# Two-layer hybrid attention trunk on one core: warm-up products of 512 rounded columns, values of two head pairs in one group, and a new written-out order

## The chip, the cores and the metric

The kernel runs on one core of one Trainium2 chip. The metric is the device time of one execution in microseconds (us). Of the kernel before there are three timed executions and one profiled one.

## The reference, cut to what matters

A trunk of two layers on 256 tokens of 1024 features. Layer 0 feeds two groups of heads from one projection: A (8 heads, sliding window with sinks) and B (8 heads, three branches: compressed, selected, window). Layer 1 is block-sparse attention with 16 heads. With 256 tokens every selected block and every window covers all earlier tokens, so each of these branches is causal attention here. The values of B are the sum of three gated branches for each head:

```python
for layer in range(DEPTH):
    ada = silu(c) @ w_ada[layer] + b_ada[layer]
    shift, scale, gate = split(ada, 3)
    h = rms_norm(x, norm_g[layer]) * (1 + scale) + shift
    y = even_mixer(h, ...) if layer % 2 == 0 else odd_mixer(h, ...)
    x = x + gate * y
return rms_norm(x, final_g)

# even_mixer, B:
o = g[..., 0:1] * o_cmp + g[..., 1:2] * o_slc + g[..., 2:3] * o_win   # then * silu(zb), then w_out
```

## The kernel before, in words

Every product with weights is made in rounded fp32 (float32r) from split operands: ScalarE rounds a weight tile to `whi` (a cast), VectorE subtracts to get the rest `wlo`, activations are split in the same way into `hhi`/`hlo` and `ghi`/`glo`, and `mm3` (line 557) makes three products of each pair: high by high, high by low, low by high. Attention scores, values, transposes and the small adaLN products are in plain fp32; a plain fp32 product that is no transpose shows as two records in the trace.

`Plan` (line 183) records each instruction with its number instead of issuing it (so nearly every row of the profile has the line of the call in `record`, L276). `issue` (line 279) then issues all of them in the order of the table `ORDER`, written out by hand at the top of the file; each engine's own queue is the part of that table that belongs to it. `FLIP` lists by number the copies and scalings that go to the other one of VectorE and ScalarE. An engine works through its queue in order. The DMAs of the weights are all issued from SP.

The stages, in order of time:

- Start (lines 356 to 381 and 685 to 823). 32 warm-up products of a 128x128 tile of ones (`ones`, lines 369 to 378) stand in TensorE's queue between the first small products; nobody reads their result. Shift and scale of layer 0 are made in five groups of feature blocks (`START`, line 24). For each, DMAs bring a part of `w_ada` into tiles that are free at that time (`qT`, `gate`, `oT`, `kTb`, `t`), VectorE adds up the first few of its rows into `acc`, and TensorE adds the rest in a group of tiled products into bank `ps_m` (`start_sums`, line 731). With shift and scale of a block known, the block of the normed input is split, and `start_mm` (line 793) multiplies it with its rows of `w_in_even`, which come through `raw` tiles.
- Layer 0 attention (lines 834 to 1114). `attn_four` (line 609) makes the scores of two heads and two branches (`ps_s`), VectorE takes row extremes (`mn`), ScalarE the exponentials (`sm`, `den`), VectorE the reciprocals (`rc`), either of them scales, TensorE transposes (`ps_pt`), and the copies land in tiles of the ring `pT`, which has 4 tiles and 3 more out of `bigA`. `attn_values` (line 660) then multiplies with the values into bank `ps_o`; `plan.group` makes each of its products wait for what any of them needs. `b_pair` (line 1054) does this for the two heads of one pair: ten products, twenty records, one bank, one gating (`gated`) of 256 columns. Between them stand projections for the SiLU gates (`gate_path`), the compression MLP (`compress`), and VectorE's adaLN sums for later (`fill`, tiles `raw` and `acc`).
- Output projection of layer 0 and norm for layer 1 (lines 1116 to 1150), then layer 1 (lines 1152 to 1289) and its output projection, norm and stores (lines 1290 to 1330).

## Time and profile before

| | us |
|---|---|
| median of 3 runs (294.68, 294.72, 314.98) | 294.72 |
| the profiled execution | 295.43 |
| its span from first to last instruction | 293.7 |
| mean granted TensorE clock over the span | 0.996 |

The profile is of the execution that took 295.43 us; 1.73 us of that lie outside its span. In the profile PE is TensorE's matmul, PEld its weight load, DVE is VectorE, ACT ScalarE, POOL GpSimd, and SPq the queue that SP issues DMAs from. A row `ps_o<-pT,vb x16` stands for sixteen records that write a tile of `ps_o` from `pT` and `vb`; buffer numbers are left out. The time of a matmul record holds its own latency and overlaps the next one, so the pace is read from the starts, not from the durations.

### The profile page before, as it was taken

The page shows a single profiled execution, that of the slowest core. Times are in us where ns is not written, and L with a number is a line of the kernel's source. Part 1 is how long each engine was busy: PE and PEld are TensorE (multiplying, and loading weights), DVE is VectorE, ACT ScalarE, POOL GpSimd, SP SyncE. Part 2 cuts the span into 40 slices and gives each one's busy share as a digit, 9 for nine tenths or more (in the row PEclk, how much of TensorE's full clock was granted, in tenths as well). Part 3 has the DMA queues.
Part 4 walks back from the last instruction along what each step waited for, and adds up shares of the span by engine and source line. Part 5 has one row for each costly group of instructions (what it writes and reads, how often), then busy time and mean ns, then how long its engine had stood idle before and what let it go on. Part 6 is the DMA issues. An engine that isn't in the chain of part 4 may idle for free.

```text
span 293.7 us, 6077 instructions
## 1 busy us (share of the span) xinstructions
PE 283.5 (97%) x2244; PEld 243.5 (83%) x2244; DVE 253.0 (86%) x612; ACT 201.2 (69%) x513; POOL 5.5 (2%) x27
## 2 busy tenths in 40 slices
PE   8989999999999999999899999999999999999991
PEld 7868888997789888777667799999799899887891
DVE  0669999999999999999899868898699889889973
ACT  5554746695999999996398744466667377783821
POOL 2100000000000000000000000000000000000000
PEclk9999999999999999999999999999999999999998
DMA  7999999987996787799996449608927661604003
GB/s 260 364 385 377 383 355 353 311 287 237 342 400 212 264 281 293 213 323 361 305 372 216 146 143 329 243 4 296 351 71 249 237 234 34 227 27 145 1 15 129
DMA packets 50557, 71.76 MB, mean 244 GB/s; under 512 B 2792, under 2 KB 36192, under 8 KB 50528
## 3 DMA queue, kind: packets, MB, share of 16 engines
q1 hardware_dynamic: 50128, 70.95, 70.7%
q10 hardware_dynamic: 400, 0.43, 0.4%
q8 instruction: 17, 0.28, 0.4%
q14 instruction: 12, 0.10, 0.1%
HBM read 70.32 MB, written 1.06 MB: 243 GB/s over the span
## 4 chain that ended last, share of the span: by engine, by line
PE 73%; DVE 13%; DMA 8%; issue 2%; ACT 2%; SPq 0%; DVEq 0%
PE ps_pj L276 49%; PE ps_s L276 9%; PE ps_pt L276 6%; DVE raw L276 5%; PE ps_o L276 4%; PE ps_m L276 4%; DMA kTb<-in_w_ada_dram 3%; DMA raw<-in_w_ada_dram 2%; DVE wlo L276 2%; DMA qT<-in_w_ada_dram 2%; DMA xs<-in_x_dram 1%; DVE t L276 1%; DVE oT L276 1%; ACT t L276 1%; DVE bigA L276 1%
## 5 line engine op out<-in xcount | busy, mean ns | idle before, releaser
L276 ACT CAST whi<-raw 128x512 fp32r<-128x512 f32 (+2 forms) x108 | 71.6, 689 | 33.6 <-PE ps_pj L276 15.8
L276 DVE TENSOR_TENSOR wlo<-raw,whi 128x512 fp32r<-128x512 f32 (+2 forms) x92 | 70.8, 792 | 6.4 <-ACT whi L276 6.4
L276 PE MATMUL ps_pj<-hlo,whi 128*128 128x256 f32 x256 | 70.8, 284 | 0.0
L276 PE MATMUL ps_pj<-hhi,wlo 128*128 128x256 f32 x256 | 70.0, 284 | 0.3 <-DVE wlo L276 0.3
L276 PE MATMUL ps_pj<-hhi,whi 128*128 128x256 f32 x256 | 69.9, 284 | 0.0
L276 PEld LDWEIGHTS ps_pj<-hlo,whi 128*128 128x128 f32 x256 | 48.0, 189 | 0.6 <-issue 0.3
L276 PEld LDWEIGHTS ps_pj<-hhi,wlo 128*128 128x128 f32 x256 | 47.4, 189 | 0.7 <-DVE wlo L276 0.5
L276 PEld LDWEIGHTS ps_pj<-hhi,whi 128*128 128x128 f32 x256 | 47.4, 188 | 0.3
L276 ACT ACTIVATE sm<-sm,mn 128x256 f32<-128x256 f32 (+1 forms) x58 | 25.9, 449 | 6.9 <-DVE mn L276 6.9
L276 PE MATMUL ps_pj<-whi,hhi 128*128 128x512 f32 (+2 forms) x72 | 25.8, 368 | 0.5 <-ACT hhi L276 0.4
L276 PE MATMUL ps_pj<-whi,hlo 128*128 128x512 f32 (+2 forms) x72 | 26.1, 374 | 0.0
L276 PE MATMUL ps_pj<-wlo,hhi 128*128 128x512 f32 (+2 forms) x72 | 26.0, 370 | 0.0
L276 DVE SCALAR_TENSOR_TENSOR wlo<-raw,whi 128x512 fp32r<-128x512 f32 x32 | 20.6, 686 | 3.7 <-ACT whi L276 3.6
L276 PE MATMUL ps_pj<-wlo,ghi 128*128 128x512 f32 (+1 forms) x56 | 20.4, 368 | 0.0
L276 PE MATMUL ps_pj<-whi,ghi 128*128 128x512 f32 (+1 forms) x56 | 20.4, 369 | 0.0
L276 PE MATMUL ps_pj<-whi,glo 128*128 128x512 f32 (+1 forms) x56 | 20.0, 367 | 0.0
L276 ACT ACTIVATE sm<-sm,rc 128x256 f32<-128x256 f32 (+1 forms) x41 | 17.3, 449 | 2.3 <-DVE rc L276 2.3
L276 DVE SCALAR_TENSOR_TENSOR raw<-raw,cz,raw 128x1024 f32<-128x1024 f32 x14 | 17.9, 1276 | 1.0 <-DMA raw<-in_w_ada_dram 0.9
L276 DVE SCALAR_TENSOR_TENSOR acc<-raw,cz,acc 128x1024 f32<-128x1024 f32 x14 | 17.9, 1278 | 0.1
L276 PEld LDWEIGHTS ps_pj<-whi,hhi 128*128 128x128 f32 x72 | 13.6, 188 | 2.7 <-ACT hhi L276 1.2
L276 PEld LDWEIGHTS ps_pj<-whi,hlo 128*128 128x128 f32 x72 | 13.5, 188 | 2.5 <-DVE hlo L276 0.8
L276 PE MATMUL ps_pt<-ident,sm 128*128 128x128 f32 x87 | 15.5, 279 | 0.0
(252 smaller groups left out, 599.7 us busy)
## 6 DMA issues: line engine op xcount, KB each, us to landing
raw<-in_w_in_odd_dram SPq DMA_DIRECT2D x16, 1024.0 KB, 7.5
raw<-in_w_ada_dram SPq DMA_DIRECT2D x8, 1024.0 KB, 6.2
raw<-in_w_ada_dram SPq DMA_DIRECT2D x16, 512.0 KB, 5.2
raw<-in_w_in_even_dram SPq DMA_DIRECT2D x8, 652.0 KB, 7.2
raw<-in_w_in_even_dram SPq DMA_DIRECT2D x5, 1024.0 KB, 7.7
raw<-in_w_out_even_dram SPq DMA_DIRECT2D x4, 1024.0 KB, 5.4
raw<-in_w_out_odd_dram SPq DMA_DIRECT2D x4, 1024.0 KB, 5.0
qT<-in_w_ada_dram SPq DMA_DIRECT2D x12, 256.0 KB, 6.2
```

What stands on the lines that cost most here:

```text
L276: self.ops.append(dict(key=eng.key, deps=deps, fn=lambda: getattr(real, name)(*args, **kw)))
```

## The change

It has four parts.

1. The warm-up products are made in rounded fp32 and with 512 columns instead of 128, from the first 512 columns of `ghi`, which is set to one for it by VectorE (a memset of 128x512 in place of one of 128x128). Their number, 32, stays. `ones` shrinks to two columns.
2. `b_quad` takes the place of two calls of `b_pair`: the scores and softmax of two head pairs are recorded, then all their values, twenty products, in one group into the two halves of one bank, then one gating of 512 columns. Four groups of values become two. The `stop` flag is now set for each half.
3. `pT_more` makes the ring of `pT` tiles one longer (8 in layer 0); `hp` has one buffer instead of two.
4. `ORDER` and `FLIP` are written anew, so that instructions on all engines stand in another order. The numbers in it also shift by one from the eighth instruction on. By `FLIP`, eleven copies and scalings more are VectorE's and eleven fewer ScalarE's; with one memset more and two gatings fewer VectorE has 624 instructions for 614, ScalarE 422 for 433. Four of the eleven are scalings of 128x128 in layer 0's attention.

```diff
 ORDER = [int(i) for i in """
-49 7 6 4 0 1 9 21 22 23 2 3 47 5 91 41 42 48 92 89 24 25 26 27 28 29 30 93 73 88 50 31 90 32 74 99 58 33 75 34
...
+2944 2916 2919 2917 2872 2945 2946 2947 2948 2973 2974 2975 2976 2977 2980 2982 2981 2983 2978 2979
...
-    ones = const([P, P], "ones")
+    ones = const([P, 2], "ones")
+    ghi = const([P, KT, S], "ghi", F32R)
+    ones_r = ghi[:, 0:2, :].rearrange("p a b -> p (a b)")
     ring_warm = bank("m")
+    V.memset(ones_r.bitcast(F32), 1.0)
     V.memset(ones, 1.0)
     dummy = const([P, 2], "dummy")
     A.activation(dummy[:, 0:1], ones[:, 0:1], AF.Exp)
     for _ in range(WARM):
-        T.matmul(ring_warm[:, :P], ones, ones, start=True, stop=True)
+        T.matmul(ring_warm, ones_r[:, :P], ones_r, start=True, stop=True)
     keep = bank("o")
     for _ in range(20):
-        T.matmul(keep[:, :P], ones, ones, start=True, stop=True)
+        T.matmul(keep, ones_r[:, :P], ones_r, start=True, stop=True)
...
-    ghi = const([P, KT, S], "ghi", F32R)
     glo = const([P, KT, S], "glo", F32R)
...
         ids = []
+        last = {cs: n for n, (cs, keys) in enumerate(jobs)}
...
-                        stop=n == len(jobs) - 1 and m == len(keys) - 1,
+                        stop=n == last[cs] and m == len(keys) - 1,
...
     bigA = const([P, 2304], "bigA")
+    pT_more = const([P, 3 * P], "pT_more")
...
-            hp = sb([P, 256], "hp", 2)
+            hp = sb([P, 256], "hp", 1)
...
-        ks = sb([P, 256], "hp", 2)
+        ks = sb([P, 256], "hp", 1)
...
+    ring["pT"][0].append(pT_more)
...
-    def b_pair(hp_, cmp):
+    def b_pair(hp_):
         g = hp_ // 2
...
         pts = attn_four([keys(0), keys(1)], maskc, None, [gv[:, 2 * hp_ : 2 * hp_ + 2, :, 1 + br] for br in range(2)])
+        cs = S * (hp_ % 2)
+        return [(cs, cmp_keys(hp_))] + [(cs, keys_of(lambda b, br=br: vb[:, b, 3 * br + g, :], pts[br])) for br in range(2)]
+
+    def b_quad(g, mid):
+        js = b_pair(2 * g)
+        mid()
+        js += b_pair(2 * g + 1)
         po = bank("o")
-        attn_values(po, ([(0, cmp_keys(hp_))] if cmp else []) + [(0, keys_of(lambda b, br=br: vb[:, b, 3 * br + g, :], pts[br])) for br in range(2)])
-        gated(po, 4 + hp_, 1, 0.25)
-        if hp_ % 2:
-            gated_parts(3 + hp_)
-
+        attn_values(po, js)
+        gated(po, 4 + 2 * g, 2, 0.25)
+        gated_parts(4 + 2 * g)
...
-    b_pair(0, True)
-    fill(1)
-    b_pair(1, True)
+    b_quad(0, lambda: fill(1))
     fill(1)
     gate_path(W0, 2456 + 256, 6)
-    b_pair(2, True)
-    fill(1)
-    fill(1)
-    b_pair(3, True)
+    b_quad(1, lambda: fill(2))
     fill(1)
     fill(1)
```

The first place is the start, on TensorE: the rows before the second `ps_m` group of `start_sums` (tiles `kTb`, `oT` with `cz` and `acc`), which shifts and scales feature blocks 1 and 2. `whi`, `wlo`, `hhi` are split weights and inputs of block 0. Before:

```order
L276 MATMUL ps_pt_90<-whi_113,hhi 128x256
L276 MATMUL ps_o_70<-wlo_117,hhi 128x408
L276 MATMUL ps_pj_100<-whi_112,hhi 128x512
L276 MATMUL ps_pt_90<-wlo_117,hhi 128x256
L276 MATMUL ps_s_98<-ident,t_94 128x128
L276 MATMUL ps_pj_101<-wlo_116,hhi 128x512
L276 MATMUL ps_pj_100<-wlo_116,hhi 128x512
L276 MATMUL ps_s_97<-wlo_116,hhi 128x512
L276 MATMUL ps_m_68<-kTb,cz 32x128 x8
L276 MATMUL ps_m_68<-acc_111,cz 32x128 x4
```

And of the changed kernel, where a warm-up product reads `ghi`:

```order
L275 MATMUL ps_s_98<-whi_113,hhi 128x512
L275 MATMUL ps_o_71<-ghi 128x512
L275 MATMUL ps_pj_102<-whi_113,hhi 128x512
L275 MATMUL ps_o_71<-ghi 128x512
L275 MATMUL ps_pj_101<-whi_113,hhi 128x512
L275 MATMUL ps_s_99<-whi_113,hhi 128x512
L275 MATMUL ps_m_69<-oT,cz 32x128 x8
L275 MATMUL ps_m_69<-kTb,cz 32x128 x8
L275 MATMUL ps_m_69<-acc_112,cz 32x128 x4
L275 MATMUL ps_s_99<-wlo_117,hhi 128x512
L275 MATMUL ps_s_98<-wlo_117,hhi 128x512
```

Before, thirteen products of block 0 stand ahead of that group (the seven of them above and six earlier ones; together 5472 columns: six products of 512, four of 408, three of 256); now four of 512 columns do (2048 columns), all of them above, and the others stand behind it. The `oT` part of the group has moved down to the `kTb` part.

What SP issues in that time, before (`xs` is the input, `raw` holds rows of `w_in_even`; a row of 128x1304 is 652 KB, 128x384 is 192 KB, the `w_ada` pieces 256 KB each):

```order
L276 DMA xs<-in_x_dram 128x1024 x2
L276 DMA qT_104<-in_w_ada_dram 128x4x128
L276 DMA raw_106<-in_w_in_even_dram 128x1304
L276 DMA qT_103<-in_w_ada_dram 128x4x128
L276 DMA raw_106<-in_w_in_even_dram 128x384
L276 DMA qT_103<-in_w_ada_dram 128x4x128
L276 DMA qT_104<-in_w_ada_dram 128x4x128
L276 DMA oT<-in_w_ada_dram 128x2x256 x2
L276 DMA qT_105<-in_w_ada_dram 128x2x256 x2
L276 DMA gate<-in_w_ada_dram 128x2x256 x2
L276 DMA kTb<-in_w_ada_dram 128x2x256 x2
L276 DMA raw_107<-in_w_in_even_dram 128x1304
```

And now:

```order
L275 DMA xs<-in_x_dram 128x1024
L275 DMA gate<-in_w_ada_dram 128x2x256
L275 DMA qT_106<-in_w_ada_dram 128x2x256 x2
L275 DMA xs<-in_x_dram 128x1024
L275 DMA qT_104<-in_w_ada_dram 128x4x128 x2
L275 DMA qT_105<-in_w_ada_dram 128x4x128 x2
L275 DMA raw_107<-in_w_in_even_dram 128x1304
L275 DMA gate<-in_w_ada_dram 128x2x256
L275 DMA kTb<-in_w_ada_dram 128x2x256
L275 DMA oT<-in_w_ada_dram 128x2x256 x2
L275 DMA kTb<-in_w_ada_dram 128x2x256
L275 DMA raw_107<-in_w_in_even_dram 128x384
```

The second half of the input and the first weight rows go behind pieces of `w_ada`, and the 192 KB of `raw` that stood in the middle go behind the last piece of `kTb`.

The second place is layer 0's B heads. On TensorE, the values of the second pair before (`pcT` are the compressed branch's weights, `pT` and `bigA` the transposed softmax tiles, `vz` and `vb` the values):

```order
L276 MATMUL ps_pj_99<-whi_114,glo 128x512
L276 MATMUL ps_pt_90<-ident,sm_127 128x128 x3
L276 MATMUL ps_o_70<-pcT,vz 64x256 x2
L276 MATMUL ps_o_70<-bigA,vb 64x256
L276 MATMUL ps_o_70<-pT_131,vb 64x256
L276 MATMUL ps_o_70<-bigA,vb 64x128
L276 MATMUL ps_o_70<-pT_131,vb 64x128
L276 MATMUL ps_o_70<-pT_132,vb 64x256
L276 MATMUL ps_o_70<-pT_133,vb 64x256
L276 MATMUL ps_o_70<-pT_132,vb 64x128
L276 MATMUL ps_o_70<-pT_133,vb 64x128
L276 MATMUL ps_s_97<-kTb,qT_103 128x128
```

And the first half of the first quad's values now; the second half, ten more products, follows at once:

```order
L275 MATMUL ps_pj_101<-whi_115,glo 128x512
L275 MATMUL ps_pt_91<-ident,sm_128 128x128 x2
L275 MATMUL ps_o_71<-pcT,vz 64x256 x2
L275 MATMUL ps_o_71<-pT_133,vb 64x256
L275 MATMUL ps_o_71<-pT_134,vb 64x256
L275 MATMUL ps_o_71<-pT_133,vb 64x128
L275 MATMUL ps_o_71<-pT_134,vb 64x128
L275 MATMUL ps_o_71<-pT_135,vb 64x256
L275 MATMUL ps_o_71<-bigA,vb 64x256
L275 MATMUL ps_o_71<-pT_135,vb 64x128
```

And on ScalarE now, from the copy that fills the last tile the first quad needs (`pT_132`) to the copy that can start only when the quad's values have been made, since it writes a tile that they read (`pT_133`):

```order
L275 COPY pT_132<-ps_pt_91 128x384
L275 ACTIVATE bigA,den_141<-bigA,mn_138 128x256
L275 ACTIVATE sm_130,den_140<-sm_130,mn_137 128x256
L275 ACTIVATE bigA,den_141<-bigA,mn_138 128x128
L275 ACTIVATE bigA,den_141<-bigA,mn_138 128x256
L275 ACTIVATE oT<-ps_pj_100 128x512
L275 ACTIVATE oT<-ps_pj_102 128x512
L275 CAST whi_116<-raw_110 128x1024
L275 ACTIVATE bigA<-bigA,rc_144 128x256
L275 ACTIVATE sm_130<-sm_130,rc_143 128x128
L275 ACTIVATE sm_131<-sm_131,rc_143 128x256
L275 COPY pT_133<-ps_pt_91 128x384
```

Before, the group of ten products stood between scores of one pair and the next, and a copy of the following pair wrote a tile freed one pair earlier; now one tile less is free at that point.

## Rows read from the trace of the kernel before

**Rows 1.** The page: engines over the whole span.

```profile
PE 283.5 (97%) x2244; PEld 243.5 (83%) x2244; DVE 253.0 (86%) x612; ACT 201.2 (69%) x513; POOL 5.5 (2%) x27
```

**Rows 2.** Windows: length, busy PE, PEld, DVE, ACT, POOL; clock; DMA; GB/s.

```profile
18.60:50.00 31.40, 31.39 (x238) 26.43 (x239) 28.14 (x62) 17.75 (x39) 0.00 (x0) 1.00 1.07 368
50.00:102.00 52.00, 52.00 (x463) 44.82 (x461) 51.12 (x169) 45.24 (x142) 0.38 (x3) 1.00 0.88 299
102.00:125.00 23.00, 23.00 (x196) 18.22 (x196) 23.00 (x54) 22.79 (x67) 0.32 (x1) 1.00 0.75 255
125.00:146.00 21.00, 20.63 (x121) 15.55 (x119) 19.94 (x34) 14.39 (x34) 0.00 (x0) 1.00 0.95 328
146.00:166.00 20.00, 18.86 (x90) 13.20 (x90) 18.01 (x43) 17.22 (x42) 0.61 (x2) 1.00 0.82 280
166.00:287.40 121.40, 121.35 (x996) 110.75 (x996) 102.79 (x228) 72.85 (x172) 0.95 (x3) 1.00 0.48 162
```

**Rows 3.** Waits of PE over the whole span: total us, times, longest.

```profile
PE ps_m L276 <- DMA kTb<-in_w_ada_dram: 1.1, 1, 1.1
...
PE ps_s L276 <- DVE wlo L276: 0.8, 1, 0.8
PE ps_pj L276 <- ACT hhi L276: 0.4, 1, 0.4
PE ps_pj L276 <- DVE wlo L276: 0.3, 1, 0.3
```

**Rows 4.** The chain that ended last: start, length, what.

```profile
11.01 7.55 DMA kTb<-in_w_ada_dram
18.61 0.86 PE ps_m L276 x24
...
166.05 18.91 PE ps_pj L276 x152
...
266.63 20.82 PE ps_pj L276 x112
```

**Rows 5.** Timeline of the start, and one window of it.

```profile
0.90 0.17 DVE L276 MEMSET ones<- 128x128 f32 x1 [0.90 <-PEq L1386]
...
1.49 3.86 PEld L276 LDWEIGHTS ps_o<-ones 128*128 128x128 f32 x20
...
7.23 0.49 DVE L276 TENSOR_SCALAR t<-xs,r 128x512 f32<-128x512 f32 x1
...
9.45 0.75 PEld L276 LDWEIGHTS ps_m<-ones 128*128 128x128 f32 x6
...
0.00:18.56 18.56, 16.25 (x145) 14.56 (x145) 7.61 (x19) 10.15 (x19) 3.17 (x18) 1.00 0.95 328
```

**Rows 6.** Timeline of PE around one pair's values.

```profile
135.69 0.40 PE L276 MATMUL ps_pj<-wlo,ghi 128*128 128x512 f32 x1
135.93 0.40 PE L276 MATMUL ps_pj<-whi,glo 128*128 128x512 f32 x1
136.26 0.65 PE L276 MATMUL ps_o<-pcT,vz 128*64 128x256 f32 x4
136.74 1.47 PE L276 MATMUL ps_o<-pT,vb 128*64 128x256 f32 x16
138.14 0.50 PE L276 MATMUL ps_s<-whi,glo 128*128 128x512 f32 x1
138.48 0.40 PE L276 MATMUL ps_s<-whi,ghi 128*128 128x512 f32 x1
```

**Rows 7.** Groups by form, 70 to 146 us, DVE, then ACT: busy us, mean ns.

```profile
L276 DVE SCALAR_TENSOR_TENSOR oT<-ps_o,oT 128x256 f32<-128x256 f32 x4 | 1.7, 419 | 0.0
L276 DVE SCALAR_TENSOR_TENSOR oT<-ps_o,oT 128x512 f32<-128x512 f32 x2 | 1.4, 688 | 0.0
...
L276 DVE TENSOR_SCALAR sm<-sm,rc 128x128 f32<-128x128 f32 x2 | 0.6, 280 | 0.0
L276 ACT CAST whi<-raw 128x1024 fp32r<-128x1024 f32 x12 | 12.4, 1043 | 2.3 <-PE ps_pj L276 2.0 <-DMA raw<-in_w_out_even_dram 0.3
L276 ACT ACTIVATE sm<-sm,mn 128x256 f32<-128x256 f32 x15 | 7.5, 503 | 2.3 <-DVE mn L276 2.3
```

257 rows, old and new, of tables (FLIP, ORDER) are left out of this document.

## The prediction

> **What bounds the kernel now.** I read the page's first part, the windows by stage, the waits of TensorE, the chain that ended last, and then the timeline where a step needs a pace. The page gives PE 97% of the span [rows 1]. The windows say what stands beside it: from 18.6 to 125 us PE is full, and from 50 to 125 us VectorE is full with it, 74.1 of 75 us [rows 2]. From 166 to 287.4 us PE is full alone, and VectorE has 18.6 us to spare. The waits of PE are few: 1.1 us for the DMA of `kTb` in the start, and 0.8, 0.4 and 0.3 us for VectorE and ScalarE [rows 3]. The chain fits: a DMA until 18.56 us, then TensorE's work, and from 166.05 to 287.45 us TensorE's again [rows 4]; between them it goes through VectorE.
>
> So layer 1 can give nothing but by fewer products, and the change takes none of these away. What can move is the start before 18.6 us, the amount of TensorE's and VectorE's work from there to 166 us, and about 1.5 us of waits at the layer's end.
>
> **Warm-up products.** They go from 32 plain products of 128 columns, 64 records, to 32 rounded ones of 512. At the later pace an old record takes 0.11 us: six loads take 0.75 us with the last one's own latency in it [rows 5]. That is 64 x 0.11 = 7.0 us. A rounded product of 512 columns takes 0.24 us from start to start [rows 6], so 32 x 0.24 = 7.7 us. In the first 4 us records stand 3.86 / 20 = 0.19 us apart on average [rows 5], and the new products should be slower in the same ratio; the page's granted clock shows no step there. The difference lies between 0 and 0.7 us. The memset before the first of them grows from 0.17 us; four times that is 0.66, an operation of VectorE over 128x512 took 0.49 [rows 5], so it is up to 0.5 us later. I cost both at nothing: the cover is the wait of the second `ps_m` group for `kTb`, which becomes longer than its 1.1 us by the products that no longer stand ahead of it. Without that cover they cost up to 1.2 us.
>
> **Start, the new order.** Behind 18.6 us PE is never idle until 125 us, so a product that was made before that group and is now made after it is time lost, unless the group comes sooner. Nine products of block 0 move behind it, 5472 - 2048 = 3424 columns: 3424 / 512 x 0.24 = 1.6 us later. What comes sooner: up to the last piece of `kTb` SP issued 4,940 KB (1,024 of `xs`, 12 x 256 of `w_ada`, 652 + 192 of `raw`), and now 4,748 KB, since 192 KB of `raw` go behind it. At 368 GB/s [rows 2] that is 0.53 us. But when `kTb` had landed, 18.56 us x 328 GB/s = 6.1 MB had moved [rows 5], 1.0 MB more than what was issued up to it, so transfers behind it had run beside it, and the gain can be as little as 0. The trace has no row between; I take the middle, 0.3.
>
> The Trainium skill (page "DMA: Bandwidth & Descriptors", section "Queues, rings and completion order") says that completion is not in the order of issue for one issuing engine. By that the group comes no sooner and the start costs 1.6 us; by strict order it would cost 1.1. The 6.1 MB agree with the page.
>
> The second half of the input is issued behind 768 KB of `w_ada`. Its square and scaling come later, but its transposes stand behind the first `ps_m` group now, and the wait for `kTb` is behind them too: nothing. Sum for the start: 1.6 - 0.3 = +1.3 us.
>
> **Values in one group.** One pair's values take 1.88 us, 136.26 to 138.14. Ahead of them the start-to-start time is 0.33 us where 0.24 is the pace, behind them 0.34: 0.09 + 0.10, so 0.2 us for entering and leaving a group [rows 6]. Four groups become two: -0.4 us of PE. The products themselves stay.
>
> On VectorE four gatings of 256 columns at 0.419 us become two of 512 at 0.688: -0.3 us. Four scalings of 128x128 come over from ScalarE at 0.28 each: +1.1 [rows 7]. So VectorE has 0.8 us more in a stretch in which it is full, and ScalarE four instructions less.
>
> TensorE is then 1.3 - 0.4 = 0.9 us later at the layer's end and VectorE 0.8 us. They run side by side, so I count the later one, +0.9, not the sum. If the two hit each other instead of lying side by side, it is up to 1.7.
>
> **A buffer more for `pT`, one less for `hp`.** A copy into `hp` now waits until the two small products that read the tile are done. The trace shows no such wait; two products of 512 columns would be 0.5 us, and 0 is the other end. Behind it on ScalarE wait exponentials and casts for TensorE. I take 0, because TensorE has products of a projection in its queue there and never waits from 50 to 102 us. The first copy for the third pair must wait for the whole first quad. In the order ScalarE has ten instructions between the two copies: four exponentials at 0.5, one cast at 1.04 and five more at about 0.5 by the nearest rows, 5.6 us, and 0.5 for the copy before [rows 7]. TensorE needs for its part three products of 256 columns, a set of scores, three transposes, two products of 512, some 2 us, and the values, 2 x 1.88: 5.8 us. ScalarE comes there no sooner than the tile is free: 0.
>
> **Layer's end.** The 1.5 us of waits of PE at 125 to 166 us [rows 3] are for splits of the new input and of weights. Both orders interleave the transposes with the last output products, the new one with six products between the last transposes and the second token half's first product, where there were four. I take off the 0.4 us for `hhi` and leave the others; the ends are -1.5 and +0.5.
>
> **Sum.** +0.9 - 0.4 = +0.5 us, on the profiled execution's 295.43: 295.9. The median is 0.7 below that execution, so the forecast is 294.72 + 0.5 = 295.2 us.
>
> **Rivals.** First, the waits go: TensorE finds other work ready in the start, since VectorE has 3.3 us and ScalarE 13.7 us to spare from 18.6 to 50 us [rows 2], the start's loss shrinks to its order's 0.3 us or less, and the 1.5 us of waits at the layer's end go. 294.72 + 0.3 - 0.4 - 1.5 = 293.1 us. For it speaks that all of these waits are single ones; against it that nine products plainly stand behind the group.
>
> Second, slower: the third pair's first copy holds ScalarE. If ScalarE reaches it before TensorE has made the first quad's values, it stands there for up to their 3.8 us, and behind it are the casts of the output projection's weights, for which VectorE and then TensorE wait. It decides from the point where ScalarE's ten instructions take less than TensorE's 5.8 us; they are equal within 0.3 us by my count. ScalarE is at 22.8 of 23 us in that stretch, so most of such a hold is lost: 294.72 + 0.5 + 3.3 = 298.5 us.
>
> Third, the pace of PE itself. In the stretch from 166 us weight loads fill 110.75 of 121.4 us, 91%; from 18.6 to 166 us they fill 118.2 of 147.4, 80% [rows 2]. If an order could bring that stretch to 91%, it would take 118.2 / 0.91 = 129.9 us, 17.5 less: 277.2 us. Against it: products of 512 columns follow each other at 0.24 us without a gap [rows 6], and the stretch has the small tiled products, whose loads are short. The Trainium skill (page "Perfetto Trace Analysis", section "Identifying the Most-Contended Engine") holds that matmul busy time says little of the distance to the roof and that the busy share of weight loads is the better measure. By that rule the 97% would hide 17% to be had; the starts in this trace do not bear it out here.
>
> **Chances and range.** The forecast, between 294 and 297 us: 0.50. The waits go: 0.27. ScalarE is held: 0.16. The pace of PE: 0.02. The rest, 0.05, is slower than all of these, as by a clock that falls in the longer wait before 18.6 us or by all upper bounds together (1.2 + 0.3 + 0.8 + 0.5 + 0.9 us more). About 2%, 5.9 us, is what a measurement of this kernel can tell from no change. Below 288.8 us lies the third rival and a little of the first, 0.03; above 300.6 us the rest and a tail of the second, 0.06; within, 0.91. The range for 8 in 10 reaches from 292.2, the first rival with the lower bounds of the layer's end, to 298.4, just short of the second.
>
> **What would show it.** In the changed kernel's timeline the second `ps_m` group should start at 18.1 to 18.6 us after a wait of PE of over 2 us, with four products of block 0 ahead of it. One gap-free set of forty records should stand for each quad's values, some 3.8 us long. VectorE should be full from 50 to 125 us again, and PE's stretch for layer 1 about 121 us long, from some 166.5 us on. The forecast is wrong if that last stretch begins before 165 or after 169 us, if ScalarE shows a wait for `ps_o` or `pT` of over 1 us near 108 to 114 us, or if the clock shows a step after 5 us.

## The result and the profile after

The changed kernel takes 299.41 us (median of 6 executions, 298.9 to 300.86), the kernel before 294.7 on the same chip: a ratio of 1.0172, with a 95% interval from 1.0145 to 1.0199. One of the six executions of the kernel before, at 314.98 us, is not in that ratio; the medians alone give 1.016. The forecast was 295.2, and its range ended at 298.4. So the change costs 4.7 us, where I had given it 0.5.

The page of the changed kernel shows PE as full as before:

```profile
PE 287.5 (97%) x2212; PEld 243.0 (82%) x2212; DVE 255.9 (86%) x622; ACT 197.6 (66%) x502; POOL 6.3 (2%) x27
```

It has 32 records fewer [rows 1], those of the old warm-up, and 4.0 us more of busy time. The windows of [rows 2], cut at the same times, so that the work in them has shifted, and the start:

```profile
18.60:50.00 31.40, 30.94 (x218) 25.66 (x213) 27.30 (x59) 17.26 (x37) 0.00 (x0) 1.00 1.07 366
50.00:102.00 52.00, 51.95 (x453) 44.68 (x454) 50.66 (x173) 46.46 (x143) 0.45 (x3) 1.00 0.89 297
102.00:125.00 23.00, 23.00 (x205) 18.67 (x204) 23.00 (x60) 22.70 (x69) 0.32 (x1) 1.00 0.74 260
125.00:146.00 21.00, 21.00 (x119) 15.97 (x118) 19.17 (x30) 12.14 (x29) 0.00 (x0) 1.00 0.87 300
146.00:166.00 20.00, 19.01 (x91) 13.41 (x90) 17.39 (x37) 16.14 (x35) 0.89 (x2) 1.00 0.75 249
166.00:287.40 121.40, 120.95 (x979) 108.75 (x978) 104.69 (x233) 72.73 (x173) 0.96 (x2) 1.00 0.53 171
0.00:18.56 18.56, 16.41 (x128) 11.88 (x128) 8.04 (x20) 7.93 (x15) 3.27 (x18) 1.00 0.93 307
```

From 125 to 146 us PE is busy for all 21.0 us and makes 119 records; before it was busy for 20.63 and made 121. A busy engine is not one at its pace. The last line shows the start: 307 GB/s instead of 328 [rows 5]. The waits of TensorE, against [rows 3]:

```profile
PE ps_o L275 <- DVE ghi L275: 1.5, 1, 1.5
PE ps_pj L275 <- DVE hlo L275: 0.7, 2, 0.4
PE ps_pj L275 <- DVE t L275: 0.4, 1, 0.4
PE ps_m L275 <- DMA qT<-in_w_ada_dram: 0.4, 1, 0.4
```

The wait for `kTb` is gone, no wait is long behind the first (the memset at the very beginning), and still the time is longer. So the waits don't tell where it went. What does is progress: from the trace's records I counted the columns of the rounded weight products (437,376 in all) and noted when each count is reached. Lag in us behind the profiled execution before, one execution of each kernel; the runs named are those of the next section:

```
columns done         first  20000  80000  110000  170000  240000    last
before, at           14.20  26.35  56.98   88.03  139.87  178.33  287.16
after                +1.58  +1.68  +2.10   +2.57   +4.03   +4.00   +4.15
e1_alternate         +2.12  +1.55  +1.95   +2.42   +2.55   +2.26   +2.41
e4_old_order         +0.65  +0.12  +0.42   +0.42   +3.50   +2.47   +2.36
e5_warm              +0.74  +0.46  +0.59   +0.60   +0.45   -0.63   -0.59
e6_quads             +0.04  -0.50  -0.38   -0.38   +2.75   +1.72   +1.63
f3_warm_aligned      +0.16  +0.31  +0.38   +0.40   +0.28   +0.38   +0.24
f4_before_shifted    +0.45  +0.23  +0.48   +0.47   +0.37   +0.16   +0.03
e11_three_fewer      +0.10  +0.02  +0.13   +0.15   +0.06   +0.14   +0.00
e12_before_fewer     -0.40  -0.23  -0.14   -0.15   -0.18   -0.73   -0.81
f5_before_aligned    +0.19  +0.40  +0.33   +0.46   +0.91   +0.66   +1.48
g1_before_256        -0.04  -0.41  -0.46   -0.33   -0.19   -0.25   +0.59
e7_start_and_tiles   +0.99  +0.32  +0.50   +2.39   +2.72   +2.74   +2.90
e8_new_start         +0.88  +1.59  +1.72   +3.86   +3.80   +3.58   +3.49
g2_wide_ones_tiles   +1.30  +0.80  +1.25   +1.73   +1.73   +2.03   +2.18
```

1.7 us are lost by 20,000 columns, in the start, 0.9 more up to 110,000, and 1.5 up to 170,000, in the second half of layer 0's attention. The layer's end and layer 1 add 0.1. The stretch from 80,000 to 110,000 columns as a window, before and after:

```profile
56.98:88.03 31.05, 31.05 (x304) 26.23 (x304) 30.58 (x109) 26.95 (x88) 0.38 (x3) 1.00 0.89 306
59.08:90.60 31.52, 31.47 (x303) 26.49 (x302) 30.76 (x109) 28.55 (x89) 0.45 (x3) 1.00 0.91 299
```

TensorE is full in both and makes as many records but one, and still takes 0.5 us longer. That is the new order's: e1 and g2, which have it, lose the same 0.5 us there, and e4, the same program in the old order, loses nothing. In the new order TensorE's queue goes from one kind of product to another 79 times in this stretch, in the old one 63 times (weight products of one width are one kind, the others go by operands and shape). But a change has no fixed price: from 110,000 to 170,000 columns e1 changes 146 times for 110 before and loses 0.1 us. So the cause of the 0.5 us stays open.

Of the start, the changed kernel's timeline:

```profile
9.12 1.06 ACT L275 ACTIVATE t<-xs 128x1024 f32<-128x1024 f32 x1 [3.40 <-DMA xs<-in_x_dram]
...
11.35 0.49 DVE L275 TENSOR_SCALAR t<-xs,r 128x512 f32<-128x512 f32 x1 [2.29 <-POOL r L275]
...
14.20 1.14 ACT L275 CAST whi<-raw 128x512 fp32r<-128x512 f32 x2 [1.47 <-DMA raw<-in_w_in_even_dram]
...
15.79 0.50 PE L275 MATMUL ps_s<-whi,hhi 128*128 128x512 f32 x1 [0.24 <-ACT hhi L275]
...
17.37 0.65 PE L275 MATMUL ps_m<-oT,cz 128*32 128x128 f32 x16
```

ScalarE stands 3.40 us for the second half of the input and 1.47 for the first weights, both issued later now, and the first weight product comes at 15.79 us instead of 14.20. The second `ps_m` group comes at 17.37, 1.24 sooner than the 18.61 of [rows 4], and not at 18.1 to 18.6. And of the second quad's values, first and last records:

```profile
135.58 0.65 PE L275 MATMUL ps_o<-pcT,vz 128*64 128x256 f32 x4
136.07 0.82 PE L275 MATMUL ps_o<-pT,vb 128*64 128x256 f32 x8
...
139.81 0.81 PE L275 MATMUL ps_o<-pT_more,vb 128*64 128x256 f32 x4
140.56 0.50 PE L275 MATMUL ps_pj<-wlo,ghi 128*128 128x512 f32 x1
```

From the first to the product behind the group it is 140.56 - 135.58 = 4.98 us for forty records; the first quad's took 3.61 (120.55 to 124.16), and two pairs took 3.76 before [rows 6].

### The profile page after: what moved, and what is told of

The parts are those of the page before. It is cut to its first block, busy times and chain, and to the rows that moved or that the text cites. A ratio compares the mean times of both kernels' runs of the same rounds, so it can differ in the third digit from the quotient of the medians.

```text
span 297.6 us, 6011 instructions
## 1 busy us (share of the span) xinstructions
PE 287.5 (97%) x2212; PEld 243.0 (82%) x2212; DVE 255.9 (86%) x622; ACT 197.6 (66%) x502; POOL 6.3 (2%) x27
## 4 chain that ended last, share of the span: by engine, by line
PE 61%; DVE 19%; DMA 11%; ACT 4%; issue 2%; ACTq 0%; SPq 0%; DVEq 0%; POOL 0%
PE ps_pj L275 43%; PE ps_s L275 7%; DVE raw L275 5%; PE ps_pt L275 5%; DMA raw<-in_w_in_even_dram 5%; DVE wlo L275 4%; PE ps_o L275 3%; PE ps_m L275 3%; DMA t<-in_w_ada_dram 3%; DMA raw<-in_w_ada_dram 2%; ACT t L275 2%; DVE t L275 2%; DVE xs L275 2%; DMA rows<-in_b_ada_dram 2%; DVE acc L275 1%
## 5 line engine op out<-in xcount | busy, mean ns | idle before, releaser
L275 ACT CAST whi<-raw 128x512 fp32r<-128x512 f32 (+1 forms) x108 | 71.2, 690 | 30.8 <-PE ps_pj L275 22.9
L275 PEld LDWEIGHTS ps_pj<-hlo,whi 128*128 128x128 f32 x256 | 47.3, 188 | 0.5 <-issue 0.3
L275 ACT ACTIVATE sm<-sm,mn 128x128 f32<-128x128 f32 (+1 forms) x58 | 26.0, 451 | 6.7 <-DVE mn L275 6.7
L275 PE MATMUL ps_pj<-whi,hhi 128*128 128x512 f32 (+2 forms) x72 | 26.4, 373 | 0.7 <-ACT whi L275 0.4
L275 DVE SCALAR_TENSOR_TENSOR wlo<-raw,whi 128x512 fp32r<-128x512 f32 x32 | 21.2, 684 | 3.2 <-ACT whi L275 3.2
L275 ACT ACTIVATE sm<-sm,rc 128x256 f32<-128x256 f32 (+1 forms) x37 | 16.0, 456 | 0.3 <-DVE rc L275 0.2
```

The lines of the kernel that those rows point to most:

```text
L275: self.ops.append(dict(key=eng.key, deps=deps, fn=lambda: getattr(real, name)(*args, **kw)))
```

## Experiments

Medians are given with the ratio to the kernel before, timed beside it (294.4 to 294.7 us in every comparison).

**The order of the value products (e1, e2, e3).** In the table the second quad's products of one head stood together; e1 lets the heads alternate:

```
-1399 1401 1403 1405 1400 1407 1409 1411 1413 1402 1404 1406 1408 1410 1412
+1399 1400 1401 1402 1403 1404 1405 1406 1407 1408 1409 1410 1411 1412 1413
```

> The changed kernel, with one edit: the 20 value products of the second head group's two pairs stand so that the two heads (column tiles 0 and 64) alternate, as they do in the first group. Theory of the column tiles: in the trace of the changed kernel the alternating group's forty records take 3.61 us and the other group's 4.97, so this returns 4.97 - 3.61 = 1.36 us, and the time falls from 299.4 to 298.0, with the second group at 3.6 us. Rival, VectorE: it is busy 19.2 of 20 us from 125 to 146 us in the changed kernel, so that the group's 1.4 us would come back as a wait for VectorE within the next 10 us: 299.4, with a new TensorE wait of over 1 us behind the group.

298.27 us, 1.0140 (1.0114 to 1.0166), 1.1 us less than the changed kernel, though the two intervals overlap. The same group in its timeline, to the product behind it:

```profile
135.46 0.65 PE L276 MATMUL ps_o<-pcT,vz 128*64 128x256 f32 x4
135.94 1.03 PE L276 MATMUL ps_o<-pT,vb 128*64 128x256 f32 x9
...
139.07 0.50 PE L276 MATMUL ps_pj<-wlo,ghi 128*128 128x512 f32 x1
```

3.61 us, like the first quad; no wait behind it. The theory of the column tiles holds and the rival falls. e2 and e3 put the start back into its old order, e3 with e1's edit:

```
-ORDER, FLIP of the changed kernel
+ids below 477 in the order and on the engines of the kernel before
```

> The changed kernel, with the work of the start (up to about 60000 columns of weight products, some 50 us, on all five engines) in the order and on the engines of the kernel before, the new warm-up products of 512 columns in the places of the old ones; everything behind it as in the changed kernel. Theory of the start's order: the changed kernel lags by 1.6 us at its first weight product and by 1.8 to 2.1 us from 30000 columns on, all of it from the order in which transfers are issued and work stands, so 299.4 - 2.0 = 297.4, the first weight product at about 14.2 us. Rival, the warm-up products themselves (eight of them 0.43 us apart, a memset of 0.48 us before them, PE held longer before the first transposes): they keep the lag in the old order too, 299.0 to 299.4, the first weight product at 15.5 or later.

> The edits of the two runs before together. If the start's order and the column tiles are two separate costs, 299.4 - 2.0 - 1.36 = 296.0, and what stays above the 294.7 of the kernel before, 1.3 us, is in neither. Rival, one cost hides the other (the second half of layer 0's attention is paced by VectorE, whatever TensorE starts with): 297.4 to 298.0, no faster than the better of the two alone.

304.10 and 303.05 us, 1.0328 and 1.0286. Both miss: where the two orders meet, near 50 us, a new wait stands in e2,

```profile
PE ps_pt L276 <- DVE wlo L276: 3.7, 1, 3.7
```

so these two say nothing of the start beyond that point. They differ by e1's edit alone, and by 1.05 us, which agrees with e1.

**Program and order apart (e4, e5, e6).** e4 is the changed program in the old order, e5 the new warm-up alone, e6 the groups and buffers alone, both in the old order:

```
 e4: -ORDER, FLIP of the changed kernel   +those of the kernel before, renumbered
 e5: -T.matmul(ring_warm[:, :P], ones, ones, ...)   +T.matmul(ring_warm, ones_r[:, :P], ones_r, ...)
 e6: -b_pair(0, True); fill(1); b_pair(1, True)     +b_quad(0, lambda: fill(1))
```

> The program of the changed kernel (warm-up products of 512 columns, values of two pairs in one group, one buffer less and one more) with every engine's instructions in the order of the kernel before; the first pair's value products stand right ahead of the second's, as the group needs. Theory that the new order alone costs: within 0.5 us of the kernel before, 294.2 to 295.2. Rival, that the changed program costs of itself (a first product 0.5 us later by the memset and long warm-up products, ScalarE held for the third pair's copies): 296 to 298.

> The kernel before with the warm-up alone changed: a memset of 512 columns and 32 rounded products of 512 columns in the places of the first 32 of the old ones, the order of all else kept. In the run of the changed program in the old order the lag behind the kernel before is 0.65 us at the first weight product and 0.4 us from 50000 to 140000 columns, all that the warm-up can have cost there: 294.45 + 0.4 to 0.65 = 294.9 to 295.1. Rival, the warm-up costs nothing, as I had forecast (what it delays would be hidden by the wait for the transfer of kTb): 294.3 to 294.6, the second ps_m group no later than before.

> The kernel before with the values of two pairs in one group, hp in one buffer and the further pT buffer, in the old order (the first pair's value products right ahead of the second's), the old warm-up. In the run of the changed program in the old order the lag grows by 2.0 us between 145000 and 185000 columns, with a TensorE wait of 1.3 us for ScalarE's copy into bigA and one of 1.0 us for VectorE's oT; if that is the group's own, 294.45 + 2.0 to 3.0 = 296.5 to 297.5 with the same two waits. Rival, the group costs nothing or gains its 0.4 us where VectorE is the bound: 294.0 to 294.6.

297.95 us, 1.0121 (1.0100 to 1.0142); 295.26 us, 1.0024 (1.0008 to 1.0041); 297.07 us, 1.0084 (1.0069 to 1.0098). The program costs without any new order, and its two parts add up to the whole within the intervals. In e6 the loss is in two waits of TensorE, each shown behind the instruction that ends it:

```profile
117.02 0.69 DVE L276 SCALAR_TENSOR_TENSOR oT<-oT,ps_pj 128x512 f32<-128x512 f32 x1
...
117.76 0.50 PE L276 MATMUL ps_pj<-whi,ghi 128*128 128x512 f32 x1 [1.01 <-DVE oT L276]
...
131.15 0.41 ACT L276 ACTIVATE bigA<-bigA,rc 128x128 f32<-128x128 f32 x1
...
131.62 0.55 PE L276 MATMUL ps_pt<-ident,bigA 128*128 128x128 f32 x3 [1.33 <-ACT bigA L276]
```

A product waits for VectorE to read its bank (a multiplication of the gate path, not the quad's gating), and transposes wait for the scaling of the tile that they read, which stands behind a cast and a copy in ScalarE's queue. The new order has neither wait, but as a whole it gains nothing: e4, the same program in the old order, is faster than the changed kernel (the intervals don't overlap) and no slower than e1. And e6 shows something of the kernel before: its start has that kernel's order, and it has no wait for `kTb` and lies 0.4 to 0.5 us ahead of the profiled execution from 20,000 to 110,000 columns.

**The start's order (e7 to e10).** e7 is e3 with the seam further on, where the first attention begins; e8 is the other way round, the kernel before with the changed start:

```
 e7: -ids below 477 in the old order   +ids below 716 in the old order
 e8: -ORDER, FLIP of the kernel before   +ids below 715 in the new order
```

> The changed kernel with the start in the order and on the engines of the kernel before up to about 98000 columns (ahead of the first attention, a later seam than in the run with 60000, whose own wait of 3.7 us at the seam hid the answer), and the second head group's value products alternating. Theory of two separate costs: the lag of 2.1 us at 98000 columns shrinks to the warm-up's 0.4, and the column tiles give their 1.1: 299.4 - 1.7 - 1.1 = 296.6. Rival, the attention behind the start is paced by VectorE and gives the start's gain back: 298.2, as with the alternating products alone.

> The kernel before, its start alone (up to about 98000 columns, all engines) in the order and on the engines of the changed kernel; the old warm-up products. If the order of the start costs by itself (the first weight transfer is issued at 6.8 us instead of 2.2, the second half of the input later), 294.45 + 1.6 = 296.1, the first weight product at 15.2 or later. Rival, the start is late in the changed kernel because of the long warm-up products ahead of the transposes: 294.3 to 295.0, the first weight product within 0.5 us of 14.2.

298.47 us, 1.0131 (1.0115 to 1.0147), and 298.25 us, 1.0120 (1.0102 to 1.0139). By the medians the first is no better than e1 and the second far worse than expected; the lags say why. At 80,000 columns the old start stands at +0.50 against e1's +1.95, and the new one at +1.72 against -0.38 in e6: the new order of the start costs 1.5 to 2.1 us, by one execution of each. In e8, with the old warm-up, the first weight product comes 0.88 us later; in e5, with the new warm-up in the old order, 0.74; together that is the changed kernel's 1.58. Up to 110,000 both lose some 2 us more where the orders meet. So neither median measures the start alone. e9 and e10 exchange only SyncE's first sixteen transfers, a set that both kernels share, in e1 and in the kernel before:

```
-3 98 95 96 4 89 90 91 92 93 97 101 99 100 102 94
+4 3 92 93 90 94 89 91 100 99 95 96 98 97 102 101
```

> The changed kernel with the alternating value products, and SyncE's first 16 transfers (input, the first weights, the first tiles of w_ada) in the order of the kernel before; nothing else moved. Theory of the transfers: ahead of its seam the run with the old start lags 0.5 us at 80000 columns, the one with alternating products alone 1.95; if those 1.45 us hang on the order of the first transfers (the first weight piece issued at 6.8 us there and at 2.2 in the kernel before), 298.3 - 1.45 = 296.8, the first weight product near 15 us instead of 16.3. Rival, they hang on the order on the other engines, built for the new transfers (VectorE's acc<-qT stands ahead of the input's second half there and would now wait for its tile): 298.3 or slower.

> The kernel before with SyncE's first 16 transfers in the order of the changed kernel; nothing else moved. Theory of the transfers: 294.6 + 1.5 to 2.1 = 296.1 to 296.7, by the lags of 1.7 us at 80000 columns with the whole new start and of -0.4 with the old start. Rival, the order of the transfers alone costs under 0.5 us (all 16 must land before the second ps_m group anyway): 294.6 to 295.1.

302.29 us, 1.0280, and 299.25 us, 1.0172 (1.0153 to 1.0192). Each got a single long wait of TensorE in the start, of 3.2 us for VectorE's `t` in e9 and this one in e10:

```profile
10.85 0.27 PE L276 MATMUL ps_pt<-ident,rows 64*128 64x64 f32 x1 [3.36 <-DVE tiny L276]
```

Behind both the granted clock fell, to a mean of 0.79 from 16 to 24 us in e9 and from 8 to 16 us in e10, so these two times include a slower clock. The order of the transfers and that of the engines' queues are made for each other; e9's rival held, both expectations of e10 missed, and the two cannot be priced apart by exchanging one.

**What the warm-up costs (e11, e12, f2 to f5, g1, g2).** First, fewer products:

```
 e11: e5 with    -WARM = 12   +WARM = 9
 e12: before with -WARM = 12   +WARM = 6
```

> The kernel before with the changed warm-up, as in the run of the warm-up alone (295.3), but with three products fewer, those right ahead of the first ps_m group: 29 instead of 32. Theory that the warm-up is work on the path: TensorE has no gap from its first product to the first ps_m group, which came at 11.84 us there and at 11.10 in the kernel before; three products of 0.24 us less put it at 11.1 and the time at 295.3 - 0.7 = 294.6. Rival, the cost is the late beginning (the memset ends at 1.46 us instead of 1.07, products of 0.43 us ahead of the first transpose, which comes at 6.25 us instead of 5.48) or the later landing of the transfers: 295.3, the group at 11.1 and a wait behind it.

> The kernel before with six warm-up products fewer (26 instead of 32, 12 of 64 records of 0.11 us), those right ahead of the first ps_m group. Theory that the warm-up is work on the path: the group moves from 11.1 us towards 9.8 and the time falls by up to 1.3 us, to between 293.3 and 294.0. Rival, the group then waits for its own tiles of w_ada (in the changed kernel it waited 0.4 us for qT until 12.6 us), or the first weight product for its cast: no change, 294.4 to 294.7, with a new TensorE wait ahead of the group or of the first product; with a lower granted clock behind that wait it would be slower.

295.74 us, 1.0050 (1.0031 to 1.0070), and 294.66 us, 1.0014 (0.9996 to 1.0032). No gain in either; in e12 TensorE waits 0.6 us for `qT` ahead of the first `ps_m` group and 1.1 for `hhi` at 21.3 us, behind the second. The rivals held: by the medians the products are not on the path. (In e11's execution the first weight product comes 0.64 us sooner than in e5's, but in f3's, with all 32 products, it comes 0.57 sooner as well.) But the windows of all these runs fell into two kinds: with the tile `ones` 2 columns wide the transfers moved less from 8 to 16 us. The tile had shrunk by 480 bytes in each partition, and with it every later buffer had moved. f4 moves them in the kernel before by 32 bytes, f3 and f2 move them back to multiples of 64 in e5 and e1, f5 puts `oT`, `kTb` and `gate` there too:

```
 f4: -ones = const([P, P], "ones")   +ones = const([P, P + 8], "ones")
 f3, f2: -ones = const([P, 2], "ones")   +ones = const([P, 16], "ones")
 f5: +pad_a = const([P, 8], "pad_a")   +pad_b = const([P, 8], "pad_b")
```

> The kernel before with the tile ones 136 columns wide instead of 128 (the products read the first 128 as before): 32 bytes more in each partition, nothing else. Theory of the addresses: raw, t and qT now lie 32 bytes past a multiple of 64, so 294.5 + 0.7 = 295.2, with 315 to 350 GB/s from 8 to 16 us and 355 to 373 from 30 to 40. Rival, the address means nothing: 294.5, with the rates of the kernel before (358 to 380, and 387).

> The kernel before with the changed warm-up (295.3), the tile ones 16 columns wide instead of 2, which puts the buffers of the weights back on multiples of 64 bytes. Theory of the addresses: 294.4 to 294.7, with 358 GB/s or more from 8 to 16 us and 387 or more from 30 to 40. Rival, the rounded products of 512 columns: 295.3, with 315 to 350 GB/s from 8 to 16 us as in the run of the warm-up alone.

> The changed kernel with the alternating value products (298.3) and the tile ones 16 columns wide instead of 2, 32 bytes more in each partition. By the built programs' addresses the change from 128 columns to 2 had moved every later tile by 480 bytes, so that the buffers of the weights and most buffers of w_ada (raw, t, qT) lie at 32 bytes past a multiple of 64 and not on one; the 32 bytes put them back. Theory of the addresses: in every run with the narrow tile the transfers moved 315 to 350 GB/s from 8 to 16 us and 355 to 373 from 30 to 40, in every run with the wide one 358 to 380 and 387 to 393; the start, which waits for transfers, gets back what the warm-up alone had cost in the old order, 0.7 us, or up to the 2.0 us of the whole start: 296.3 to 297.6, with over 360 GB/s from 8 to 16 us. Rival, the rounded products themselves slow the transfers or the start: 298.3, the rates as they were.

> The kernel before with two unused tiles of 32 bytes, one ahead of oT and one behind bigA, so that oT, kTb and gate, which lie 32 bytes past a multiple of 64 there and take 2 MB of the start's transfers, lie on one too, and raw, t and qT stay on one. Theory of the addresses: the transfers into those three, about a third of the bytes ahead of the second ps_m group, go up to a tenth faster, and the start gains 0.2 to 0.5 us: 294.0 to 294.3, faster than both kernels. Rival, TensorE does not wait for them in most executions (no wait for kTb stands in the run of the groups alone, whose start is that of the kernel before): 294.5.

f4: 295.46 us, 1.0028 (1.0011 to 1.0044); f3: 295.69, 1.0040 (1.0025 to 1.0056); f2: 298.29, 1.0135; f5: 296.93, 1.0086 (1.0069 to 1.0103). The kernel before with nothing changed but 32 unused bytes loses what the warm-up lost, by the medians. Multiples of 64 repair nothing, and f5 lost its own rate by them: its `raw` and `qT`, which had lain on a multiple of 256, were 64 past one. The windows (rate at the end of the line) of e6, whose buffers lie as before, and of f4:

```profile
8.00:16.00 8.00, 8.00 (x101) 7.23 (x101) 5.16 (x13) 5.24 (x11) 0.47 (x1) 1.00 1.11 370
30.00:40.00 10.00, 10.00 (x74) 8.56 (x72) 9.52 (x19) 5.51 (x14) 0.00 (x0) 1.00 1.06 393
```

```profile
8.00:16.00 8.00, 8.00 (x101) 7.21 (x101) 4.78 (x12) 4.81 (x11) 0.62 (x2) 1.00 1.12 333
30.00:40.00 10.00, 10.00 (x73) 8.51 (x69) 9.13 (x19) 5.24 (x12) 0.00 (x0) 1.00 1.07 370
```

The DMA engines are as busy (1.11 and 1.12) and move a tenth less. In the old start all nine runs with `raw` and `qT` 32 or 64 bytes past a multiple of 256 moved 333 or 334 GB/s from 8 to 16 us, and the runs with both on one 366 to 375. The start follows: at 80,000 columns the four executions of the old start with the old places (before, e6, e12, g1) lag by -0.46 to 0 us, the seven with moved ones (e4, e5, e7, e11, f3, f4, f5) by 0.13 to 0.59. The whole time doesn't follow this alone: f4 and f5 moved the same 333 and 334 GB/s and lie 1.5 us apart. The last two runs use multiples of 256:

```
 g1: before with four unused tiles: oT, kTb, gate, t, qT, raw all on multiples of 256
 g2: e1 with   -ones = const([P, 2], "ones")   +ones = const([P, P], "ones")
```

> The kernel before with four unused tiles (640 bytes in all positions together 512) that put oT, kTb, gate, t, qT and raw all on multiples of 256 bytes; there, raw and qT lie on one already, t on a multiple of 128, oT, kTb and gate on one of 32. Theory that the offset of a buffer from a multiple of 256 (or 128) sets how fast it is written: the three runs with raw and qT 32 or 64 bytes past such a multiple moved 312 to 351 GB/s from 8 to 16 us, the kernel before and the groups alone 358 to 380; with oT, kTb and gate repaired too, the rate from 8 to 16 us rises above 380 and the start gains 0.2 to 0.5 us: 294.0 to 294.3. Rival one, only raw and qT matter, or TensorE waits for none of the three: 294.5 with the rates of the kernel before. Rival two, it is not the offset but the place in another sense: rates of 315 to 350 again, 295.3.

> The changed kernel with the alternating value products and the tile ones 128 columns wide, as in the kernel before, which puts raw, t and qT at the offsets they have there (256, 128 and 256 bytes past a multiple of 512); the 16 columns tried before had left them 64 bytes past a multiple of 256. Theory of the offsets: the start gains what the shift alone cost the kernel before, 0.8 us: 298.3 - 0.8 = 297.5, with 355 GB/s or more from 8 to 16 us and 385 or more from 30 to 40. Rival, the start in the new order has its limit elsewhere: 298.3, whatever the rate.

g1: 295.31 us, 1.0033 (1.0021 to 1.0046); g2: 298.02 us, 1.0128 (1.0107 to 1.0149). g1's window:

```profile
8.00:16.00 8.00, 8.00 (x102) 7.23 (x101) 5.24 (x13) 5.30 (x11) 0.40 (x1) 1.00 1.11 375
```

The rate is back, the highest of all, and the start no longer behind (-0.46 at 80,000 columns); yet the run is 0.8 us slower. Its profiled execution loses 0.84 us in layer 1 (-0.25 at 240,000 columns, +0.59 at the last), where nothing was meant to change, and f5 loses 0.82 there. No wait stands in it; it is the pace of TensorE. Two products that stand fifteen apart in layer 1, in the kernel before and in g1:

```profile
246.73 0.28 PE L276 MATMUL ps_pj<-hhi,whi 128*128 128x256 f32 x1
...
248.47 0.28 PE L276 MATMUL ps_pj<-hhi,whi 128*128 128x256 f32 x1
```

```profile
246.72 0.28 PE L276 MATMUL ps_pj<-hhi,whi 128*128 128x256 f32 x1
...
248.52 0.28 PE L276 MATMUL ps_pj<-hhi,whi 128*128 128x256 f32 x1
```

That is 116 ns from start to start, and 120. Over all weight products of 256 columns that follow each other in layer 1, the mean is 120.3 ns in g1 and 119.7 in f5, and 116.9 to 117.2 in the other eighteen kernels; products of 512 columns come about 5 ns sooner in g1 and f5. The unused tiles are all that g1 and f5 have of their own, so the place of tiles costs this too. Since f4, which moves all tiles behind `ones` together, keeps the pace, it should be tiles that moved against each other; which ones, no run shows. g2 moved 357 GB/s where e1 moved 343, and is 0.7 us ahead of e1 at 80,000 columns; its median is 0.25 better, within the intervals. No run beat the kernel before.

## Why the prediction was wrong

Three terms of the sum failed, and one cost stood in none. The start was put at +1.3 us and lost 2.1, because the later second half of the input and first weights, and the move of the buffers, were put at nothing. The values were put at -0.4 us and cost 1.1, because the second quad's products don't alternate. The layer's end was put at -0.4 us and gave nothing. The 0.5 us that the new order loses from 80,000 to 110,000 columns had no term. One by one:

- **Warm-up, "I cost both at nothing".** For the products that was right: three fewer gain nothing (e11). For the edit it was wrong. It costs 0.24% by itself, 0.7 us, and 32 bytes of unused space in the kernel before cost 0.28%, with the same loss of rate. That the place is the whole of it is argued from these two: no run has the new warm-up in the old order with the tiles at their old places. What failed is a step that I hadn't made: I read `ones` in the diff as what the products read, and not as the place of all tiles behind it. The Trainium skill (page "DMA: Bandwidth & Descriptors", section "How a descriptor splits into AXI transactions") says that a transaction has to start on a multiple of 256 bytes, so that a descriptor starting elsewhere fetches the bytes from the boundary below it for nothing; it says so of reading. The rates agree, with the written side here: 366 to 375 GB/s on multiples of 256, 333 and 334 at 32 and 64 bytes past one.
- **Start, "+1.3 us".** The size was too small by 0.8 to 1.2 us, and the reasons were wrong. The group came 1.24 us sooner, not 0.3, so the 3424 columns that moved behind it should nearly have been paid for. What I set at "nothing", the later second half of the input and the first weights, cost: the first weight product comes 1.6 us later, and the lag at 80,000 columns is 2.1 us, 2.5 against e6's execution of the old start. By e7 and e8 the order makes 1.5 to 2.1 of it, the place of the buffers 0.7 to 0.9 (f4 against e6, g2 against e1), all by single executions.
- **The cover, `kTb`.** I charged the wait of [rows 3] to the kernel, but it was seen in one execution. e5, e6, e12 and f4 keep the order of that start and don't show it; f5 and g1 do, with 1.4 and 0.8 us. Where it is missing, TensorE waits for `hhi` behind that group instead, at 21 to 22 us: 0.4 us in e6, 0.6 in e5, 0.7 in f4, 1.1 in e12. The same goes for the 0.8 us for `wlo`, which are 0.3 in e12 and nothing in e5. A cover that is there in some executions only is none, and the profiled one, 0.7 us above the median, had both (as has g1's, 0.6 above its own).
- **Values, "the products themselves stay".** They stay in number. In the first quad the saving came, 3.76 to 3.61 us, 0.15 of the 0.2 that I expected of each. In the second the table had parted the heads, and it took 4.98. I showed the rows of the first quad in the order and none of the second's; the list was there to be read. 1.1 us by e1's median, 1.37 by the group's own length.
- **`hp`, `pT` and ScalarE, "0".** In the new order this holds for TensorE: it has no wait for a copy from 95 to 150 us. ScalarE does stand for the second quad, 5.9 us where it stood 1.2 before, at the cast behind the gating and not at the copy that my second rival named:

```profile
141.39 0.62 ACT L275 CAST ghi<-oT 128x512 fp32r<-128x512 f32 x1 [5.87 <-DVE oT L275]
```

  TensorE has no wait of over 0.4 us behind it. In the old order the group costs 0.84%, 2.5 us (e6), but not by the rival's path either: no wait of ScalarE from 95 to 139 us is over 0.7 us, and TensorE waits for a scaling that stands behind other work in ScalarE's queue (1.33 us) and for VectorE (1.01). The rival's price of 3.3 us was near that; its path, a copy that holds ScalarE, came in neither order.
- **Layer's end, "-0.4".** From 170,000 to 240,000 columns the changed kernel's lag goes from 4.03 to 4.00, e1's from 2.55 to 2.26; but two executions of the old order differ by more there, from 1.08 us gained (e5) to 0.10 lost (f3). It can't be told from 0.
- **Sum.** The lag of 4.15 us has its places: 2.1 in the start (shown by progress and by no median, since every mixed order brought waits of its own), 0.5 between 80,000 and 110,000 columns, 1.4 in the second quad's products (1.1 by a median), 0.1 behind. That the medians differ by 4.7 us and the profiled executions by 4.1 is because the one before lies 0.7 above its median and the one after 0.1.
- **The signs I had named.** Two of those that should have come with the forecast did not: the second `ps_m` group at 18.1 to 18.6 us after a wait (17.37, without one), and a set of some 3.8 us for the second quad too (4.98). Of those that should have refuted it none came: no wait of ScalarE for a copy, no step of the clock, and the last stretch begins at 167.63 us, between 165 and 169,

```profile
167.63 26.53 PE ps_pj L275 x209
```

  but that is where a wait ends, and not how far the work is. A count of the work done would have been the better sign.

## What to carry to other kernels

Read an order to its end: two lists with the same instructions differ in time when products for different column tiles no longer alternate. A changed tile size moves every tile allocated behind it; look at the addresses of the buffers that transfers write, and compare the rate of the transfers and the pace of the products before and after. Here all buffers on multiples of 256 bytes brought the rate back and cost the pace (g1), so neither is enough by itself. And when a profiled execution is longer than the median, its single waits may be the difference, so none of them should be spent as cover.

## What the hardware showed that I had not expected

- Products for the column tiles at 0 and 64 run side by side when they alternate in the queue, and in blocks they follow each other: the same forty records take 3.61 us alternating and 4.98 in blocks. In the first quad of the changed kernel such pairs start together:

```profile
121.89 0.38 PE L275 MATMUL ps_o<-pT,vb 128*64 128x256 f32 x1
121.90 0.38 PE L275 MATMUL ps_o<-bigA,vb 128*64 128x256 f32 x1
122.11 0.27 PE L275 MATMUL ps_o<-pT,vb 128*64 128x128 f32 x1
122.12 0.27 PE L275 MATMUL ps_o<-bigA,vb 128*64 128x128 f32 x1
```

  The Trainium skill (page "TensorE: Matmul & The Clock Gate", section "The mechanism") says that matmuls start and end in the order of the program; by that a product can only share the array with its neighbours, and the trace agrees.
- The offset of a buffer in its partition sets the rate of the transfers into it: 370 GB/s from 8 to 16 us with `raw` and `qT` on a multiple of 256 bytes, 333 with all tiles 32 bytes further (f4), with equal busy shares of the DMA engines.
- The place of tiles also sets the pace of TensorE: 120 ns instead of 117 from start to start of weight products of 256 columns in g1 and f5, which moved tiles against each other by unused ones of 32 to 160 bytes.
- The same wait of 3.7 us of TensorE cost the clock in one execution and not in another. In e3 the granted clock fell to 0.50 behind it, the lower of its two levels, 1.2 GHz:

```profile
40.00:46.70 6.70, 4.51 (x36) 3.47 (x25) 3.74 (x11) 5.43 (x12) 0.00 (x0) 0.99 1.11 340
46.70:53.50 6.80, 5.27 (x25) 4.37 (x29) 4.27 (x11) 0.00 (x0) 0.00 (x0) 0.50 0.82 288
53.50:60.00 6.50, 6.50 (x48) 5.58 (x41) 5.14 (x13) 3.27 (x9) 0.00 (x0) 1.00 0.27 72
```

  In e2, with the same start, it stayed at 1.00 through that stretch.
